# A fused transformer step on one core: one split of V per chunk, other pools and a later row load in the expert stage

## The chip, the cores and the metric

The kernel runs on one core of a Trainium2 chip. The metric is the device time of one execution in microseconds; the median of three runs of the kernel before is 3129.43 us (3128.04 to 3133.86). Besides the runs there is a profile of one execution, with every instruction of the engines (TensorE or PE, VectorE or DVE, ScalarE or ACT, GpSimd or POOL, SyncE or SP) and every DMA packet.

## The reference

Two networks run one after the other on 512 tokens of width 1024, all in float32. The first mixes neighbourhood attention and a gated recurrence and then has a PEER layer, the stage that the change touches; the second is two layers of convolution, attention and feed-forward. PEER, cut to what matters:

```python
def block(t):                                   # 128 tokens, width 1024
    q = (t @ wq).reshape(128, 8, 2, 128)        # 8 heads
    s = einsum('tpcd,pckd->tpck', q, sub_keys)
    # product keys: the 16 best of 128 x 128 experts per head, idx and gate g
    a = gelu(einsum('tpkd,td->tpk', u[idx], t))
    return einsum('tpk,tpkd->td', g * a, v[idx])
```

There are 16384 experts, each with a row of U and a row of V of 1024 numbers.

## The kernel before, in words

**Two ways for one sum.** Of the four tiles of 128 tokens, tile 0 takes the 128 chosen rows of U and V of each token by indirect DMA (`gathered`): 256 loads of 128 rows, 512 KB each, interleaved u, v, u, v. A u row is multiplied with the token's hidden row and summed on VectorE (line 1161), a v row is scaled and added to `accg` (line 1166). The ring of gathered rows has five buffers, and loads run four jobs ahead.

The other three tiles (384 tokens) go densely through all experts on TensorE, in 128 chunks of 128 experts. The U stage (`ahead`, `hidden`) multiplies each chunk of U with the hidden vectors, called the moving rows of U, pool `h2`, applies gelu, and stores the result, `act`, 128 x 384, to a DRAM tensor `Ad`. At the same time the routing is computed, and the gate of every token for every expert, mostly zeros, is written to a DRAM tensor `Wd`. The V stage, in `peer` from line 1055, then computes for each chunk e `(act * gate)^T @ V[e]` and sums over all 128 chunks in six PSUM banks (3 tiles x 2 halves).

**Split products.** A float32 product is made of three matmuls: each operand is split into a high part (a copy rounded to fp32r by ScalarE) and a low part (the difference, by VectorE), and high x high, high x low and low x high are summed. One chunk of V has 18 matmuls of 512 columns: 3 tiles x 3 parts x 2 halves.

**One chunk of the V stage** (`operands`, line 1377): SP loads `act` (192 KB) and V[e] (512 KB, tile `w`). VectorE multiplies act with the gates `Wr` (line 1390), ScalarE makes vh (1391) and sh (1392), VectorE makes vl (1393) and sl (1394). Then SP issues a sixth of the next group's gates (`spread_rows`, chunks 2 to 7 of each group of 8, while a next group is left). Then line 1397 calls `split`, which allocates vh and vl of the same names anew and computes both again from `w`, at lines 134 and 136; the matmuls read this second pair.

**Order.** For TensorE, VectorE and ScalarE the V stage runs in the order in which it is written (`manual_schedule`); SP's and POOL's instructions are placed by a planner, and each queue runs in order. After the operands of chunk e come the gather jobs that are due: what is left of them at the start of the stage is spread evenly over chunks 0 to 119, in pairs of one u and one v step. Then come the products of chunk e - 4 (`OPS_LAG`). Chunks 126 and 127 are held back and multiplied at the end, tile by tile (`TAIL`).

**Memory.** Pools are opened on the left or on the right of SBUF and reuse the space of pools that were closed; a tile in reused space waits, by itself, for the last users of the tiles that it lies on. `pm` (right) holds the stage's tiles: Wr two buffers, act six, vh, vl, sh, sl six each; `w` has four buffers in another pool. `ar` (left) holds the row `gt2r`, a modulation row loaded to all partitions by SP (`rows_of`, line 368); it is read after the stage, at line 1096, where the sums are scaled and added to X, and the tiles of the following norms lie in `pt` on the right, opened when `pm` is closed.

Of the kernel before, what the change touches and what calls it, by code (L numbers as in the profile page):

```python
# [8 lines left out]
FR = mybir.dt.float32r  # L9
# [13 lines left out]
TD = S - T0  # L23
# [5 lines left out]
VBUFS = 6  # L29
# [6 lines left out]
OPS_LAG = 4  # L36
TAIL = 2
# [15 lines left out]
def run(gen):  # L53
    while True:
        try:
            next(gen)
        except StopIteration as e:
            return e.value


def steps(gen, n):
    for _ in range(n):
        yield next(gen)


def weave(*gens):

    at = [[0.0, i, g] for i, g in enumerate(gens)]
    while at:
        cur = min(at, key=lambda x: (x[0], x[1]))  # L70
        try:
            cur[0] += next(cur[2])
        except StopIteration:
            at.remove(cur)
# [18 lines left out]
class Net:  # L93
# [931 lines left out]
    def peer(self):  # L1025
        nc, p = self.nc, self.p
        hh, hl = self.h2
        mv = ([hh[:, k] for k in range(KC)], [hl[:, k] for k in range(KC)])
        first = self.proj_first(self.ws, mv, lambda i: self.normed_half(i, [(hh, hl, self.a2)], 1e-6, self.sh2))
        self.finish = None  # L1030
        for name in ("wo", "st", "hca", "y", "pn"):
            self.shut(name)
        mk = self.pool("mk")
        self.mk = mk.tile([128, 2, 2, C], F32, name="mk")
        self.mv = mk.tile([128, 2, 2, C], F32, name="mv")
        self.open_stream()
        self.Wd = self.tc.dram_tile([TD // WT, 128, 128, WT], F32, name="Wd")
        self.Ad = self.tc.dram_tile([128, 128, TD], F32, name="Ad")
        pg = self.pool("pg")
        self.rows_natural(pg)  # L1040
        sc = self.queries(mv, first)
        pq = self.pool("pq", "right")
        pa = self.pool("pa")
        dense = tuple([x[:, T0:] for x in part] for part in mv)
        ahead = self.ahead(pa, dense)
        self.chosen = None
        gather = self.gathered(pg)
        with self.tc.manual_schedule(engines={mybir.EngineType.PE}):
            weave(self.route(pq, pg, sc), steps(ahead, 128 - REST), self.until_routed(gather))
        self.shut("pq")  # L1050
        self.shut("psc")
        run(ahead)
        self.shut("pa")
        self.shut("h2")
        pm = self.pool("pm", "right")
        ar = self.pool("ar")
        for i in range(GROUP - WLATE):
            self.spread_rows(pm, 0, i)
        rows = self.rows_of(3, "gt2r", ar)
        banks = [[self.bank() for _ in range(2)] for _ in range(3)]  # L1060
        ops = {}
        held = []
        left = self.gather_left
        done = 0
        E = mybir.EngineType
        with self.tc.manual_schedule(engines={E.PE, E.DVE, E.Activation}):
            for e in range(128 + OPS_LAG):
                if e < 128:
                    ops[e] = self.operands(pm, e)
                want = left * min(e + 1, 120) // 120  # L1070
                for _ in range(done, want):
                    next(gather, None)
                done = max(done, want)
                if e >= OPS_LAG:
                    x = e - OPS_LAG
                    if x < 128 - TAIL:
                        self.products(banks, range(3), [(x, ops.pop(x))])
                    else:
                        held.append((x, ops.pop(x)))
        run(gather)  # L1080
        for t in range(3):
            self.products(banks, [t], held)
        self.shut("pm")
        pt = self.xp = self.pool("pt", "right")
        nf = pt.tile([128, D], F32, name="nf")
        nc.scalar.dma_start(nf, self.rowb(p['normf'], D))
        self.ss = ss = self.sp.tile([128, 4, 2], F32, name="ssx")
        self.xh = {}
        self.ws = [self.first_weights(p['awin'], 2304, q) for q in range(2)]
        for t in range(4):  # L1090
            sq = self.sp.tile([128, 2], F32, name="ssp")
            for h in range(2):
                b = banks[t - 1][h] if t else self.accg[:, h * 512:(h + 1) * 512]
                hs = slice(h * 512, (h + 1) * 512)
                y = pt.tile([128, 512], F32, name="y2", bufs=2)
                nc.vector.tensor_tensor(out=y, in0=b, in1=rows[:, hs], op=OP.mult)
                nc.vector.tensor_tensor(out=self.X[:, t, hs], in0=self.X[:, t, hs], in1=y, op=OP.add)
                self.square_sum(self.X[:, t, hs], sq[:, h:h + 1], pt.tile([128, 512], F32, name="sqx", bufs=2))
            r = self.rstd(sq, 1e-6)
            for h in range(2):  # L1100
                hs = slice(h * 512, (h + 1) * 512)
                nc.vector.scalar_tensor_tensor(self.X[:, t, hs], self.X[:, t, hs], r, nf[:, hs], op0=OP.mult, op1=OP.mult)
                self.square_sum(self.X[:, t, hs], ss[:, t, h:h + 1], pt.tile([128, 512], F32, name="sqx", bufs=2))
            self.unit(t, 1e-5, 4)
        self.shut("ar")
        self.shut("pg")
# [270 lines left out]
    def operands(self, pm, e):  # L1377

        nc, p = self.nc, self.p
        n, j = divmod(e, GROUP)  # L1380
        if j == 0:
            self.Wr = self.Wn
        a = pm.tile([128, TD], F32, name="act", bufs=ABUFS)
        nc.sync.dma_start(a, self.Ad[e])
        v = self.st.tile([128, 2, 512], F32, name="w", bufs=WBUFS)
        nc.sync.dma_start(v.rearrange("p a b -> p (a b)"), p['V'][e])
        vh, vl = (pm.tile([128, 2, 512], FR, name=n, bufs=VBUFS) for n in ("vh", "vl"))
        sh, sl = (pm.tile([128, TD], FR, name=n, bufs=VBUFS) for n in ("sh", "sl"))
        a3 = a.rearrange("p (b t) -> p b t", t=WT)
        self.anchor = nc.vector.tensor_tensor(out=a3, in0=a3, in1=self.Wr[:, :, e % GROUP], op=OP.mult)  # L1390
        nc.scalar.activation(vh, v, AF.Copy)
        nc.scalar.activation(sh, a, AF.Copy)  # L1392
        nc.vector.tensor_tensor(out=vl, in0=v, in1=vh, op=OP.subtract)  # L1393
        nc.vector.tensor_tensor(out=sl, in0=a, in1=sh, op=OP.subtract)  # L1394
        if j >= WLATE and e < 128 - GROUP:
            self.spread_rows(pm, n + 1, j - WLATE)
        vh, vl = self.split(pm, v, [128, 2, 512], "v", bufs=TAIL + OPS_LAG)
        return sh, sl, vh, vl

    def spread_rows(self, pm, n, i):  # L1400
# [460 lines left out]
```

## Time and profile before

| what | value |
|---|---|
| median of 3 runs | 3129.43 us |
| the profiled execution | 3129.33 us, span 3127.5 us |
| TensorE busy in the span | 2937.5 us, 94% |
| VectorE busy | 2033.6 us, 65% |
| ScalarE busy | 1387.3 us, 44% |
| moved by DMA | 544.63 MB, mean 174 GB/s |
| V stage, 1338 to 1987 us | TensorE 569.24 us, VectorE 630.78, ScalarE 314.07, 325 GB/s |

Busy time is the union of an engine's instructions. PE is TensorE's matmuls, PEld its weight loads, SPq, ACTq and POOLq the parts of an engine that issue DMAs. In a timeline or a group, `[... <-X]` or `idle before ... <-X` is the time that the engine stood idle before it and the instruction that released it. The DMA share is the time that packets took over the time of the 16 DMA engines; packets that overlap count twice. A start is in us from the first instruction.

### The profile page before, as it was taken

How to read it: one execution, taken by the hardware profiler on the slowest of the kernel's cores; microseconds unless marked ns; L12 is line 12 of the kernel's file. 1: busy time of each engine (PE TensorE's matmuls, PEld its weight loads, DVE VectorE, ACT ScalarE, POOL GpSimd, SP SyncE). 2: the span in 40 equal slices, each digit the busy share in tenths (PEclk: the TensorE clock that was granted, in tenths of full speed). 3: DMA queues.
4: the chain of work that ended last, by engine and by line, in shares of the span. 5: the costliest groups of instructions: out<-in, count | busy, mean ns of one | idle time of the engine just before them, and what ended most of it. 6: DMA issues, size and time to landing. Idle time of an engine off the chain costs nothing.

```text
span 3127.5 us, 42558 instructions
## 1 busy us (share of the span) xinstructions
PE 2937.5 (94%) x16010; PEld 2488.1 (80%) x16010; DVE 2033.6 (65%) x3768; ACT 1387.3 (44%) x2404; POOL 458.0 (15%) x399
## 2 busy tenths in 40 slices
PE   7898998999999999978888888899999999999998
PEld 5787987899998999966666666678888887788887
DVE  5744496459999867679999999644433335543323
ACT  4233563343466667844444444533322234433222
POOL 2100000000111222224444443000000000000000
PEclk9999999999999999999999999899999999999999
DMA  6622202345666778899999998222333222123332
GB/s 251 226 69 78 62 1 95 108 133 193 225 231 218 267 263 290 294 311 337 342 338 337 341 341 306 87 71 90 101 99 97 95 88 66 51 88 96 100 102 81
DMA packets 262510, 544.63 MB, mean 174 GB/s; under 512 B 21904, under 2 KB 139936, under 8 KB 257952
## 3 DMA queue, kind: packets, MB, share of 16 engines
q1 hardware_dynamic: 200096, 350.28, 34.1%
q0 software_dynamic: 36896, 134.25, 12.6%
q10 hardware_dynamic: 25312, 57.39, 5.0%
q8 instruction: 125, 2.05, 0.3%
q14 instruction: 81, 0.66, 0.1%
HBM read 489.38 MB, written 52.45 MB: 173 GB/s over the span
## 4 chain that ended last, share of the span: by engine, by line
PE 53%; DVE 23%; issue 10%; DMA 2%; POOL 1%; ACT 1%; SPq 0%; POOLq 0%; ACTq 0%; DVEq 0%
PE bank L123 51%; DVE vl L1393 4%; DVE accg L1166 3%; DVE gr L1161 3%; DVE act L1390 2%; DVE sl L1394 2%; DVE wl L1350 1%; POOL gr L1142 1%; PE bank L608 1%; PE bank L1500 1%; DVE A L826 1%; DVE KX L802 1%; DVE QX L803 0%; DMA gr<-in_Un_dram,iu 0%; DVE tmp L1240 0%
## 5 line engine op out<-in xcount | busy, mean ns | idle before, releaser
L123 PE MATMUL bank<-hh,wl 128*128 128x512 f32 (+2 forms) x2304 | 837.0, 364 | 31.7 <-DVE wl L1350 21.2
L123 PE MATMUL bank<-hh,wh 128*128 128x512 f32 (+2 forms) x2304 | 840.5, 366 | 10.8 <-ACT wh L149 4.4
L123 PE MATMUL bank<-hl,wh 128*128 128x512 f32 (+2 forms) x2304 | 834.8, 362 | 1.8 <-DVE hl L273 1.1
L150 DVE TENSOR_TENSOR wl<-w,wh 128x1024 fp32r<-128x1024 f32 (+2 forms) x280 | 295.2, 1055 | 645.9 <-ACT wh L149 639.0
L149 ACT ACTIVATE wh<-w 128x1024 fp32r<-128x1024 f32 (+2 forms) x280 | 257.4, 920 | 746.1 <-PE bank L123 602.9
L123 PEld LDWEIGHTS bank<-hh,wl 128*128 128x128 f32 x2304 | 437.8, 190 | 89.9 <-DVE wl L1350 32.3
L123 PEld LDWEIGHTS bank<-hh,wh 128*128 128x128 f32 x2304 | 436.7, 190 | 64.8 <-ACT wh L149 5.0
L123 PEld LDWEIGHTS bank<-hl,wh 128*128 128x128 f32 x2304 | 437.8, 190 | 49.2 <-DVE hl L273 1.9
L1142 POOL DMA_INDIRECT gr<-in_V_dram,iv x128 | 212.4, 1660 | 588.1 <-DVE gr L1161 546.2
L123 PE MATMUL bank<-vl,sh 128*128 128x512 f32 x768 | 247.7, 404 | 42.9 <-DVE vl L136 42.8
L123 PE MATMUL bank<-vh,sh 128*128 128x512 f32 x768 | 245.4, 401 | 36.9 <-ACT vh L134 36.9
L123 PE MATMUL bank<-vh,sl 128*128 128x512 f32 x768 | 237.9, 391 | 0.0
L123 PEld LDWEIGHTS bank<-vl,sh 128*128 128x128 f32 x768 | 137.6, 188 | 105.7 <-DVE vl L136 82.0
L123 PEld LDWEIGHTS bank<-vh,sh 128*128 128x128 f32 x768 | 139.6, 188 | 89.8 <-ACT vh L134 63.5
L1142 POOL DMA_INDIRECT gr<-in_Un_dram,iu x128 | 165.9, 1296 | 295.1 <-DVE gr L1161 158.3
L1392 ACT ACTIVATE sh<-act 128x384 fp32r<-128x384 f32 x128 | 67.3, 526 | 309.1 <-DVE act L1390 309.1
L1349 ACT ACTIVATE wh<-w 128x1024 fp32r<-128x1024 f32 x128 | 135.4, 1058 | 142.3 <-PE bank L123 133.4
L1350 DVE TENSOR_TENSOR wl<-w,wh 128x1024 fp32r<-128x1024 f32 x128 | 156.1, 1220 | 62.1 <-ACT wh L1349 62.1
L123 PEld LDWEIGHTS bank<-vh,sl 128*128 128x128 f32 x768 | 144.5, 188 | 31.3
L217 POOL TENSOR_TENSOR r<-r,mhalf 128x1 f32<-128x1 f32 x37 | 21.7, 590 | 987.2 <-DVE r L216 979.8
L1161 DVE SCALAR_TENSOR_TENSOR gr<-gr,h 128x1024 f32<-128x1024 f32 x128 | 155.9, 1219 | 15.4 <-DMA gr<-in_Un_dram,iu 15.4
L1166 DVE SCALAR_TENSOR_TENSOR accg<-gr,wt,accg 128x1024 f32<-128x1024 f32 x127 | 162.7, 1281 | 0.4
(369 smaller groups left out, 5059.2 us busy)
## 6 DMA issues: line engine op xcount, KB each, us to landing
w<-in_U_dram SPq DMA_DIRECT2D x128, 512.0 KB
w<-in_V_dram SPq DMA_DIRECT2D x128, 512.0 KB
w<-in_wgu_dram SPq DMA_DIRECT2D x84, 512.0 KB
Ad<-act ACTq DMA_DIRECT2D x128, 192.0 KB
Wd<-W ACTq DMA_DIRECT2D x24, 1024.0 KB
Wr<-Wd SPq DMA_DIRECT2D x96, 256.0 KB
act<-Ad SPq DMA_DIRECT2D x128, 192.0 KB
w<-in_wdown_dram SPq DMA_DIRECT2D x44, 512.0 KB
```

The lines of the kernel that those rows point to most:

```text
L123: return self.nc.tensor.matmul(out, a, b, start=start, stop=stop)
L149: self.nc.scalar.activation(hi[:, :, :n], w[:, :, :n], AF.Copy)
L150: (self.low or self.nc.vector).tensor_tensor(out=lo[:, :, :n], in0=w[:, :, :n], in1=hi[:, :, :n], op=OP.subtract)
L1142: nc.gpsimd.indirect_dma_start(out=t, out_offset=None, in_=table, in_offset=bass.IndirectOffsetOnAxis(ap=idx, axis=0))
L1161: nc.vector.scalar_tensor_tensor(t, t, 1.0, self.h0, op0=OP.mult, op1=OP.mult, accum_out=dots[:, h, k:k + 1])
L1166: nc.vector.scalar_tensor_tensor(acc, t, wt[:, h, k:k + 1], acc, op0=OP.mult, op1=OP.add)
L1349: nc.scalar.activation(uh, w, AF.Copy)
L1350: nc.vector.tensor_tensor(out=ul, in0=w, in1=uh, op=OP.subtract)
L1390: self.anchor = nc.vector.tensor_tensor(out=a3, in0=a3, in1=self.Wr[:, :, e % GROUP], op=OP.mult)
L1392: nc.scalar.activation(sh, a, AF.Copy)
L1393: nc.vector.tensor_tensor(out=vl, in0=v, in1=vh, op=OP.subtract)
L1394: nc.vector.tensor_tensor(out=sl, in0=a, in1=sh, op=OP.subtract)
```

## The change

The call of `split` at line 1397 is deleted, so that the pair of lines 1391 and 1393 is the one that the matmuls read. The low parts vl and sl move to a pool of their own, `pl`, opened on the right ahead of `pm` as soon as the moving rows of U (`h2`) are closed; `pm` follows it with Wr, act, vh and sh. The pool `ar` and the load of `gt2r` move from the start of the stage to behind its last gather. The number of buffers stays six each.

```diff
--- before.py
+++ after.py
@@ -1052,11 +1052,10 @@
         run(ahead)
         self.shut("pa")
         self.shut("h2")
+        self.late = self.pool("pl", "right")
         pm = self.pool("pm", "right")
-        ar = self.pool("ar")
         for i in range(GROUP - WLATE):
             self.spread_rows(pm, 0, i)
-        rows = self.rows_of(3, "gt2r", ar)
         banks = [[self.bank() for _ in range(2)] for _ in range(3)]
         ops = {}
         held = []
@@ -1078,9 +1077,12 @@
                     else:
                         held.append((x, ops.pop(x)))
         run(gather)
+        ar = self.pool("ar")
+        rows = self.rows_of(3, "gt2r", ar)
         for t in range(3):
             self.products(banks, [t], held)
-        self.shut("pm")
+        for name in ("pm", "pl"):
+            self.shut(name)
         pt = self.xp = self.pool("pt", "right")
         nf = pt.tile([128, D], F32, name="nf")
         nc.scalar.dma_start(nf, self.rowb(p['normf'], D))
@@ -1384,8 +1386,8 @@
         nc.sync.dma_start(a, self.Ad[e])
         v = self.st.tile([128, 2, 512], F32, name="w", bufs=WBUFS)
         nc.sync.dma_start(v.rearrange("p a b -> p (a b)"), p['V'][e])
-        vh, vl = (pm.tile([128, 2, 512], FR, name=n, bufs=VBUFS) for n in ("vh", "vl"))
-        sh, sl = (pm.tile([128, TD], FR, name=n, bufs=VBUFS) for n in ("sh", "sl"))
+        vh, vl = (x.tile([128, 2, 512], FR, name=n, bufs=VBUFS) for x, n in ((pm, "vh"), (self.late, "vl")))
+        sh, sl = (x.tile([128, TD], FR, name=n, bufs=VBUFS) for x, n in ((pm, "sh"), (self.late, "sl")))
         a3 = a.rearrange("p (b t) -> p b t", t=WT)
         self.anchor = nc.vector.tensor_tensor(out=a3, in0=a3, in1=self.Wr[:, :, e % GROUP], op=OP.mult)
         nc.scalar.activation(vh, v, AF.Copy)
@@ -1394,7 +1396,6 @@
         nc.vector.tensor_tensor(out=sl, in0=a, in1=sh, op=OP.subtract)
         if j >= WLATE and e < 128 - GROUP:
             self.spread_rows(pm, n + 1, j - WLATE)
-        vh, vl = self.split(pm, v, [128, 2, 512], "v", bufs=TAIL + OPS_LAG)
         return sh, sl, vh, vl
 
     def spread_rows(self, pm, n, i):
```

## Rows read from the trace of the kernel before

**Rows 1.** Stretch; busy us of PE, PEld, DVE, ACT, POOL; granted clock; DMA share; GB/s.

```profile
1400.00:1900.00 500.00, 443.58 (x1796) 327.39 (x1797) 498.58 (x629) 241.88 (x304) 222.78 (x150) 1.00 0.98 341
```

**Rows 2.** Timeline of TensorE in the tail: start us, us, line, tiles, count.

```profile
1977.34 0.61 PE L123 MATMUL bank<-vh,sh 128*128 128x512 f32 x2
...
1985.50 0.61 PE L123 MATMUL bank<-vh,sh 128*128 128x512 f32 x2
```

**Rows 3.** Groups by line, V stage: busy us, mean ns | idle before <-releaser.

```profile
L123 PE MATMUL bank<-vl,sh 128*128 128x512 f32 x768 | 247.7, 404 | 42.9 <-DVE vl L136 42.8
...
L123 PE MATMUL bank<-vh,sh 128*128 128x512 f32 x768 | 245.4, 401 | 36.9 <-ACT vh L134 36.9
...
L136 DVE TENSOR_TENSOR vl<-w,vh 128x1024 fp32r<-128x1024 f32 x128 | 156.9, 1226 | 0.0
```

**Rows 4.** Timeline of VectorE and POOL, four chunks of the V stage.

```profile
1603.19 0.55 DVE L1390 TENSOR_TENSOR act<-act,Wr 128x384 f32<-128x384 f32 x1
...
1606.43 1.22 DVE L1161 SCALAR_TENSOR_TENSOR gr<-gr,h 128x1024 f32<-128x1024 f32 x1
...
1607.92 1.74 POOL L1142 DMA_INDIRECT gr<-in_V_dram,iv  x1 [2.23 <-DVE gr L1161]
...
1608.77 0.55 DVE L1390 TENSOR_TENSOR act<-act,Wr 128x384 f32<-128x384 f32 x1
...
1612.01 0.55 DVE L1390 TENSOR_TENSOR act<-act,Wr 128x384 f32<-128x384 f32 x1
...
1614.10 1.23 DVE L136 TENSOR_TENSOR vl<-w,vh 128x1024 fp32r<-128x1024 f32 x1
...
1615.24 1.22 DVE L1161 SCALAR_TENSOR_TENSOR gr<-gr,h 128x1024 f32<-128x1024 f32 x1
```

**Rows 5.** DMA issues from 1400 to 1900 us: count, KB each, median us to landing.

```profile
w<-in_V_dram SPq DMA_DIRECT2D x100, 512.0 KB
act<-Ad SPq DMA_DIRECT2D x99, 192.0 KB
Wr<-Wd SPq DMA_DIRECT2D x72, 256.0 KB
gr<-in_V_dram,iv POOLq DMA_INDIRECT x78, 7.0
gr<-in_Un_dram,iu POOLq DMA_INDIRECT x72
```

**Rows 6.** Stretches of one group of chunks, columns as in rows 1.

```profile
1625.00:1640.00 15.00, 13.28 (x55) 10.05 (x56) 15.00 (x20) 7.87 (x11) 6.68 (x5) 1.00 1.07 356
...
1640.00:1650.00 10.00, 8.76 (x36) 6.28 (x35) 10.00 (x13) 3.69 (x6) 4.92 (x5) 1.00 1.03 399
...
1650.00:1660.00 10.00, 9.08 (x39) 6.87 (x39) 10.00 (x14) 6.03 (x8) 4.22 (x3) 1.00 0.87 287
...
1625.00:1630.00 5.00, 4.19 (x17) 3.17 (x18) 5.00 (x7) 1.84 (x4) 2.46 (x3) 1.00 1.07 326
```

**Rows 7.** Timeline of the start of the V stage [idle before <-releaser].

```profile
1332.77 4.53 SPq L1406 DMA_DIRECT2D Wr<-Wd  x6
...
1342.83 0.33 SPq L371 DMA_DIRECT2D gt2r<-Rd  x1
...
1347.64 0.56 DVE L1390 TENSOR_TENSOR act<-act,Wr 128x384 f32<-128x384 f32 x1 [15.32 <-DMA act<-Ad]
```

**Rows 8.** Chain of waits at the start of the V stage: start us, us, what.

```profile
1339.01 3.74 DMA Ad<-act
...
1343.26 4.36 DMA act<-Ad
```

**Rows 9.** Line 1386, V's loads: ns min/median/max, first and last start us.

```profile
L1386 SPq DMA_DIRECT2D w<-in_V_dram x128: 328/333/3145, 1320.4 to 1964.2; - x128
```

**Rows 10.** Timeline of VectorE at the end of the V stage.

```profile
1979.33 0.69 DVE L1096 TENSOR_TENSOR y<-accg,gt2r 128x512 f32<-128x512 f32 x1
...
1986.61 0.69 DVE L1096 TENSOR_TENSOR y<-accg,gt2r 128x512 f32<-128x512 f32 x1 [6.59 <-PE bank L123]
```

## The prediction

> **What bounds the kernel now.** I read the busy times by stretch first. Between 1400 and 1900 us, in the stage that multiplies by V, VectorE is busy 498.6 of 500 us; TensorE reads 443.6 and ScalarE 241.9 [rows 1]. A matmul's row there is longer than its pitch, since neighbours overlap, so TensorE's own pace has to come from starts: in the stage's tail, where it waits for nothing, 36 matmuls lie between the starts 1977.34 and 1985.50 [rows 2]. That is 0.227 us each, 4.08 us for the 18 of one chunk, and 522 us for 128 chunks; the stage, 1338 to 1987 us, takes 649.
>
> The groups by line then say whom TensorE waits for: 42.9 us ahead of the products with vl, released by VectorE's line 136, and 36.9 us ahead of those with vh, released by ScalarE's line 134 [rows 3]. Both lines are the second split of V: lines 1391 and 1393 have already made a pair that nobody reads. Line 136 alone is 128 x 1226 ns = 157 us of VectorE [rows 3].
>
> Last, VectorE's order in time. A chunk with a pair of gather steps runs from 1603.19 to 1608.77, 5.58 us; one without from 1612.01 to 1615.24, 3.23 us [rows 4]. In 500 us 100 V tiles are loaded and 78 + 72 = 150 rows gathered [rows 5], so 75 of 100 chunks have the pair, 6 of 8. Eight chunks are 6 x 5.58 + 2 x 3.23 = 39.9 us, as 500 us for 100 confirm. VectorE, with no gap, sets the pace of chunks 0 to 119; after that no gathers are left and TensorE runs at its own.
>
> **The second split goes.** Line 136 takes from 1614.10 to 1615.24, 1.14 us start to start [rows 4]. A chunk with gathers falls to 4.44 us, one without to 2.09; eight take 6 x 4.44 + 2 x 2.09 = 30.8 us. ScalarE's second copy lay beside VectorE's work, and an engine at 48% sets nothing before or after; it counts zero. TensorE's eight chunks are 8 x 4.08 = 32.6 us. So VectorE stops being the bound, and by these engines alone TensorE would be next, 7.3 us faster per eight chunks.
>
> **What is late next: the transfers.** The DMA engines move 341 GB/s over the 500 us, at a share of 0.98 [rows 1]. That share can't be read as full: packets overlap, and it passes 1 where the engines are pressed, 1.03 with 399 GB/s from 1640 to 1650, while the next 10 us have 0.87 with 287 GB/s [rows 6]. There is room, and I size it. A group of eight chunks moves 8 x (512 + 192) KB of V and act, 6 x 256 KB of Wr (line 1396 makes six calls) and 12 x 512 KB of gathered rows, in all 13.63 MB (sizes in [rows 5]). The 15 us with one group's Wr loads, in short packets, read 356 GB/s, 5.34 MB [rows 6]; the 3.77 MB beside Wr's 1.57 take 9.45 us at 399 GB/s, so Wr takes 5.55 us. A group needs 12.06 MB / 399 GB/s = 30.2 us plus 5.55, in all **35.8 us**: above TensorE's 32.6, below the 39.9 of now. My forecast is that the transfers become the bound and a group gains 39.9 - 35.8 = 4.1 us. Fifteen groups (chunks 0 to 119) give **62 us**.
>
> Two corrections I let cancel. Four V tiles and up to five gathered ones lie in SBUF when the stage starts, 4.7 MB or 12 us of transfer that needn't keep pace. Against it, engines kept full without a hole are an ideal: 3% lost of 15 x 35.8 us is 16 us, 5% is 27 us.
>
> [...]
>
> **Pools and the moved row load.** Today the stage begins late. SP has issued six Wr loads by 1337.3, then stands at the gt2r load, which goes out only at 1342.83 [rows 7]: its pool lies on the U stage's act tiles, whose last store (1339.01 plus 3.74 us) has to land [rows 8]. Behind it in SP's queue are the act loads; the first goes at 1343.26, lands after 4.36 us [rows 8], and VectorE's first product, at 1347.64, has waited 15.3 us for it [rows 7], with ScalarE's sh and TensorE behind. With the row load gone, act can follow Wr at 1337.3; with the same 4.36 us the first product starts at 1341.7, 6 us earlier. If the first act load must itself wait for the last store (nothing here shows whether), only the row load's place is gained, 1 us. I take **5 us**, nearer to what the chain of waits shows. vl and sl now lie on the moving rows of U, so their first writes wait for U's last matmul, a new wait; that matmul is over before the store at 1339.01, so the act tile is later still. Were it last, sl, vl and the first gather steps stand behind it on VectorE, below 1 us.
>
> At the other end SP issues gt2r behind V's last load, which goes out at 1964.2 [rows 9], and ahead of the awin weights. Its reader, line 1096, starts at 1979.33 [rows 10]: 15 us of cover for 0.33 us of issue [rows 7] and 0.52 MB / 399 GB/s = 1.3 us of transfer. Cost nothing; without cover about 5 us, as act took from issue to use. The tiles of the norm that follows now lie on vl and sl rather than on pm. Today the second y waits 6.6 us for TensorE [rows 10]; it may come free sooner, or the first one later: -3 to +1 us, taken as zero.
>
> **Sum.** 62 + 5 = 67 us off the stage; the 1140 us behind it (1987 to 3127.5) move as they are. The profiled execution took 3129.33 us for a span of 3127.5, and the median is 3129.43, so I forecast a span of 3060 and a time of **3062 us**.
>
> **Rivals.**
> A, the forecast (chance 0.60): 3045 to 3093 by the two corrections, the start and the tail.
> B, TensorE becomes the bound (0.09): 32.6 us a group, 15 x 7.3 + 5 = 115 us, time 3014. For it: the tiles loaded ahead. Against it: 13.63 MB in 32.6 us is 418 GB/s, over the 399 of the pressed stretch. [...]
> C, the long-run rate is below that of 10 us bursts (0.12): at the 356 GB/s of 1625 to 1640 a group takes 38.3 us, 15 x 1.6 + 5 = 29 us, time 3100. That row's share of 1.07 speaks for it, the 399 behind it against. [...]
> D, the gather ring becomes the wait (0.09). It has five buffers, so a V row's load goes out after the u step two pairs earlier: step at 1606.43, load at 1607.92 [rows 4], 1.49 us. It is used 1.14 us (a u step) into its own pair, so two chunks can't be shorter than landing plus 0.35 us. By the median of 7.0 us [rows 5] that is 7.4, under the 8.95 of two chunks at 35.8 us a group. If full queues push landing to 10 us, 1.4 us are lost in four chunks, 42 us in all: time 3104.
> E, slower (0.04): gathers and Wr, now always together, hold the engines at the 326 GB/s of 1625 to 1630 [rows 6]. A group takes 41.8 us, 1.9 more than now: 15 x 1.9 - 5 = 23 us lost, time 3152. It decides below 13.63 MB / 39.9 us = 342 GB/s. Against it stands the 399 of the stretch behind.
> F, no change (0.06): 341 GB/s is already the ceiling, a share of 0.98 means what it says, and only the start gains: 3124. The hole of 287 GB/s speaks against it. The second split would be gone, and VectorE would idle where it now works.
>
> A difference under 0.2%, 6 us, can't be told from none here. A to D are faster (0.90), F is the same (0.06), E slower (0.04). The range, 3014 to 3106, takes in B, C and D and leaves out E, F and a little below.
>
> **What would show it.** Lines 134 and 136 have no vh and vl left. In the same 500 us VectorE's busy share falls from 99.7% to about 86% (30.8 of 35.8), the rate rises to about 380 GB/s, and the first waits in a chunk are for landings (act, w or gr ahead of VectorE and ScalarE). VectorE's first product starts near 1342 and TensorE's last near 1919. gt2r goes out near the end. Wrong would be: about 341 GB/s with VectorE idle (E, F), VectorE waiting for gr alone beside DMA holes (D), TensorE without waits at 4.08 us a chunk (B), or a first product not before 1346.

## The result and the profile after

The changed kernel takes 3046.62 us (median of four runs, 3045.89 to 3050.66) against 3130.91 us before; the ratio is 0.9733, with a 95% interval of 0.9717 to 0.9750. The forecast was 3062 us, and the measured time lies 15 us below it, inside the range that was given. The profiled execution has a span of 3044.8 us, 82.7 less than before.

The span splits at four points: U's last matmul, VectorE's first product with act, the end of the last gather step, and the end of TensorE's last matmul with V.

| stretch, us | before | after | gained |
|---|---|---|---|
| to the start of U's last matmul | 1338.1 | 1337.4 | 0.7 |
| from there to the first product with act | 9.5 | -0.2 | 9.7 |
| from there to the end of the last gather step (chunks 0 to 119) | 603.6 | 540.3 | 63.3 |
| from there to the end of TensorE's last matmul with V | 35.8 | 34.2 | 1.6 |
| from there to the end of the span | 1140.5 | 1133.1 | 7.4 |

The forecast had 62 us for the third line, 5 for the second and nothing for the last. Busy times of the changed kernel in five stretches, with the columns of [rows 1]:

```profile
1340.00:1380.00 40.00, 40.00 (x178) 32.88 (x176) 36.46 (x50) 14.26 (x20) 18.91 (x14) 1.00 1.05 385
1400.00:1900.00 500.00, 480.56 (x2004) 369.76 (x2003) 430.69 (x581) 172.34 (x233) 221.82 (x155) 0.99 1.02 370
1400.00:1500.00 100.00, 97.12 (x412) 75.05 (x411) 88.99 (x123) 34.66 (x47) 48.55 (x34) 1.00 1.05 385
1700.00:1800.00 100.00, 94.08 (x390) 71.63 (x389) 82.10 (x113) 31.86 (x43) 45.89 (x32) 0.98 1.02 369
...
1725.00:1730.00 5.00, 5.00 (x23) 4.11 (x23) 5.00 (x8) 1.76 (x3) 3.61 (x3) 0.99 0.82 264
```

Against [rows 1] VectorE falls from 498.6 to 430.7 of 500 us, 86%, and the rate rises from 341 to 370 GB/s with the share at 1.02. In the first stretch TensorE has no hole, which fits the V tiles and gathered rows loaded ahead. Later the rate sags from 385 to 369 GB/s. The sag is made of holes: between 1700 and 1800 us the three 5 us stretches from 1725 to 1735 and from 1760 read 264, 332 and 257 GB/s, and the other seventeen average 384. Ahead of the first hole VectorE has stood 4.85 us for ScalarE's vh, which had itself waited 5.55 us for V to land:

```profile
1720.72 1.23 DVE L1395 TENSOR_TENSOR vl<-w,vh 128x1024 fp32r<-128x1024 f32 x1 [4.85 <-ACT vh L1393]
```

Meanwhile it frees no buffer: SP's loads of V wait 5.9 us for vl between 1720 and 1728, and POOL's next gather, at 1723.83, has waited 11.6 us for VectorE's u step. Who waits for whom, by groups of the stage (idle before <- releaser, as in [rows 3]):

```profile
L123 PE MATMUL bank<-vh,sh 128*128 128x512 f32 x759 | 242.9, 401 | 20.2 <-ACT sh L1394 19.4
L123 PE MATMUL bank<-vl,sh 128*128 128x512 f32 x758 | 241.1, 400 | 2.0
...
L1395 DVE TENSOR_TENSOR vl<-w,vh 128x1024 fp32r<-128x1024 f32 x128 | 156.1, 1220 | 68.1 <-ACT vh L1393 67.1 <-issue 1.0
...
L1393 ACT ACTIVATE vh<-w 128x1024 fp32r<-128x1024 f32 x127 | 133.7, 1053 | 164.3 <-DMA w<-in_V_dram 152.1 <-PE bank L123 6.9 <-issue 5.2
L1168 DVE SCALAR_TENSOR_TENSOR accg<-gr,wt,accg 128x1024 f32<-128x1024 f32 x98 | 125.4, 1280 | 4.8 <-DMA gr<-in_V_dram,iv 4.5
```

The 42.9 and 36.9 us of [rows 3] have become 2.0 and 20.2. Read from the transfers upward: ScalarE's vh waits 152 us for V to land, VectorE's vl waits 67 us for vh, and TensorE is left with 22 us of waiting. A landing now stands where VectorE's second split stood.

The start, by instruction (SP's queue, VectorE, TensorE; compare [rows 7]):

```profile
1319.72 2.45 SPq L1388 DMA_DIRECT2D w<-in_V_dram  x2
1322.26 9.54 SPq L1407 DMA_DIRECT2D Wr<-Wd  x6
1332.20 1.28 SPq L1386 DMA_DIRECT2D act<-Ad  x3
...
1337.27 0.56 DVE L1392 TENSOR_TENSOR act<-act,Wr 128x384 f32<-128x384 f32 x1 [5.62 <-DMA act<-Ad]
...
1337.45 0.34 PE L123 MATMUL bank<-hh,wl 128*128 128x384 f32 x1
1338.44 0.73 PE L123 MATMUL bank<-vh,sh 128*128 128x512 f32 x2 [0.65 <-ACT sh L1394]
...
1348.33 5.16 SPq L371 DMA_DIRECT2D gt2r<-Rd  x1
```

SP loads Wr from 1322.26, ahead of V's third tile; before it went at 1332.77, behind the fourth. So act follows at 1332.20 and TensorE goes from U to V with 0.65 us of waiting. The planner did not leave gt2r at the end: it goes out at 1348.33, in the stage's first chunks.

The end, the changed kernel first and the kernel before second (compare [rows 10]):

```profile
1903.18 0.69 DVE L1098 TENSOR_TENSOR y<-accg,gt2r 128x512 f32<-128x512 f32 x1 [3.24 <-PE bank L123]
...
1911.14 0.61 PE L123 MATMUL bank<-vh,sl 128*128 128x512 f32 x2
...
1914.40 1.00 PE L267 MATMUL bank<-ident,xh 128*128 128x128 f32 x7 [2.64 <-DVE xh L253]
```

```profile
1986.41 0.61 PE L123 MATMUL bank<-vh,sl 128*128 128x512 f32 x2
...
1996.69 1.54 PE L267 MATMUL bank<-ident,xh 128*128 128x128 f32 x6 [9.66 <-DVE xh L253]
```

The second y starts 8 us before TensorE's last matmuls, where it used to start with them. Tile 0's norm then runs beside the held products, and TensorE stands for 2.6 us behind V instead of 9.7.

### The profile page after: what moved, and what is told of

Same layout as the page of the kernel before. It is cut to its first block, busy times and chain, and to the rows that moved or that the text cites. A ratio compares the mean times of both kernels' runs of the same rounds, so it can differ in the third digit from the quotient of the medians.

```text
span 3044.8 us, 42380 instructions
## 1 busy us (share of the span) xinstructions
PE 2921.2 (96%) x16010; PEld 2493.4 (82%) x16010; DVE 1888.4 (62%) x3640; ACT 1268.0 (42%) x2276; POOL 445.7 (15%) x399
## 4 chain that ended last, share of the span: by engine, by line
PE 54%; DVE 15%; DMA 10%; issue 8%; POOL 1%; ACT 1%; SPq 0%; POOLq 0%; DVEq 0%; ACTq 0%
PE bank L123 52%; DMA w<-in_V_dram 7%; DVE accg L1168 2%; DVE vl L1395 2%; DMA Wr<-Wd 1%; DVE wl L1352 1%; DVE sl L1396 1%; DMA act<-Ad 1%; POOL gr L1144 1%; PE bank L608 1%; DVE act L1392 1%; DVE gr L1163 1%; PE bank L1501 1%; DVE KX L802 1%; DVE A L826 1%
## 5 line engine op out<-in xcount | busy, mean ns | idle before, releaser
L1144 POOL DMA_INDIRECT gr<-in_V_dram,iv x128 | 206.3, 1612 | 524.1 <-DVE gr L1163 475.6
L123 PE MATMUL bank<-vh,sh 128*128 128x512 f32 x768 | 245.6, 401 | 20.2 <-ACT sh L1394 19.4
L1144 POOL DMA_INDIRECT gr<-in_Un_dram,iu x128 | 159.7, 1248 | 298.8 <-DVE gr L1163 160.2
L1393 ACT ACTIVATE vh<-w 128x1024 fp32r<-128x1024 f32 x128 | 134.8, 1053 | 164.3 <-DMA w<-in_V_dram 152.1
L1395 DVE TENSOR_TENSOR vl<-w,vh 128x1024 fp32r<-128x1024 f32 x128 | 156.1, 1220 | 68.1 <-ACT vh L1393 67.1
```

Of the source, the lines that this page charges most:

```text
L123: return self.nc.tensor.matmul(out, a, b, start=start, stop=stop)
L1144: nc.gpsimd.indirect_dma_start(out=t, out_offset=None, in_=table, in_offset=bass.IndirectOffsetOnAxis(ap=idx, axis=0))
```

## The experiments

Each was timed beside the kernel before on the same chip. My theory: the second split made VectorE the bound, without it the transfers are, and start and tail come from pools and row load.

**One part at a time.** The first deletes the second split alone:

```diff
-        vh, vl = self.split(pm, v, [128, 2, 512], "v", bufs=TAIL + OPS_LAG)
```

> The kernel before without line 1397 alone (pools and row load as before). Theory 1 (the second split carries the stage, start and tail come from pools and row load): the stretch from VectorE's first product with act to its last gather step shrinks from 603.6 us to about 540, as in the changed kernel; the first product stays near 1347 and the stretch from the last matmul with V to the end near 1140 us; time about 3067. Rival (the start and tail gains are the split's own, since fewer VectorE and ScalarE instructions stand there): time about 3047, first product near 1337, 1133 us behind the stage.

Measured: 3067.89 us, ratio 0.9801 (0.9785 to 0.9817), as my theory had it. VectorE is as free as in the changed kernel, and the rate as high:

```profile
1400.00:1800.00 400.00, 381.91 (x1608) 295.55 (x1606) 342.75 (x469) 134.81 (x183) 184.55 (x132) 0.99 1.04 382
```

The second adds the later row load:

```diff
-        ar = self.pool("ar")
-        rows = self.rows_of(3, "gt2r", ar)
...
         run(gather)
+        ar = self.pool("ar")
+        rows = self.rows_of(3, "gt2r", ar)
```

> Line 1397 deleted and the row load moved behind the gathers, vl and sl still in pm. If the moved row load makes the start (my prediction's reason): first product near 1337 to 1342, time about 3058 to 3062, tail as before (1140 us). If the pools make it: first product still near 1346, time about 3066.

Measured: 3059.95 us, ratio 0.9781 (0.9758 to 0.9804). The time is that of the first reading; the first product, at 1347.1, is near that of the second, since U's last matmul itself came 3.6 us later in this profile than in the kernel before.

The third has the split deleted and the pools, with the row load where it was:

```diff
+        self.late = self.pool("pl", "right")
         pm = self.pool("pm", "right")
         ar = self.pool("ar")
...
+        vh, vl = (x.tile(..., name=n, bufs=VBUFS) for x, n in ((pm, "vh"), (self.late, "vl")))
+        sh, sl = (x.tile(..., name=n, bufs=VBUFS) for x, n in ((pm, "sh"), (self.late, "sl")))
```

> Line 1397 deleted and vl, sl in the pool over the moving rows of U, the row load at the start as before. If the pools carry the tail: 1133 us from the last matmul with V to the end, as in the changed kernel, whatever the start does. If they carry the start too: first product near 1337, time about 3047. If the row load carries the start: first product near 1346, time about 3055.

Measured: 3056.61 us, ratio 0.9765 (0.9748 to 0.9781). Start and tail are those of the whole change, and yet it is 10 us slower: 5 us in the gather phase, and most of the rest because U's last matmul came 4.6 us later in this profile.

The fourth is the changed kernel with the second split put back:

```diff
+        vh, vl = (x.tile(..., name=n, bufs=VBUFS) for x, n in ((pm, "vh"), (self.late, "vl")))
+        nc.scalar.activation(vh, v, AF.Copy)
+        nc.vector.tensor_tensor(out=vl, in0=v, in1=vh, op=OP.subtract)
         return sh, sl, vh, vl
```

> The changed kernel with the second split put back (V split twice, into the new pools). Theory 1: VectorE is full again, 39.9 us per eight chunks; only start (10 us) and tail (7 us) are gained: about 3113. Rival (a free buffer for each chunk's vh and vl, or the new order of SP's queue, is what sped the chunks up, not VectorE's time): about 3050.

Measured: 3118.82 us, ratio 0.9963 (0.9950 to 0.9975), 6 us above what I expected, most of it in the tail.

The fifth swaps the two pools:

```diff
-        self.late = self.pool("pl", "right")
         pm = self.pool("pm", "right")
+        self.late = self.pool("pl", "right")
```

> The changed kernel with the two pools opened in the other order: pm next to the right edge, on the moving rows of U, and pl behind it. If the start and the tail come from which tiles lie at the edge (pl there lets Wr load before V's third tile, and lets the norm's tiles start before TensorE ends): both are lost, first product about 9 us behind U's last matmul's start less the row load's 5, 1140 us behind the stage, time about 3060. If a pool of their own for vl and sl is what counts, wherever it lies: 3047.

Measured: 3058.27 us, ratio 0.9754 (0.9738 to 0.9771). The time is near the 3060 of the first reading, but half of the distance to the changed kernel is U's last matmul, 5.9 us later here.

The stretches of the first table in each of these profiles; U's last matmul starts between 1337.4 and 1343.4 in them, so the start is counted from it. That spread is older than the edits: U's first activation already starts between 684.5 and 690.2 us.

| kernel | U's last matmul to first product | gather phase | behind TensorE's end |
|---|---|---|---|
| before | 9.5 | 603.6 | 1140.5 |
| split alone | 9.9 | 537.1 | 1141.4 |
| split, row load | 5.3 | 536.9 | 1139.8 |
| split, pools | -0.4 | 545.6 | 1133.1 |
| pools, row load, V split twice | 0.3 | 603.5 | 1138.5 |
| pools in the other order | 5.1 | 540.9 | 1132.8 |
| the whole change | -0.2 | 540.3 | 1133.1 |

The columns have three causes. The gather phase belongs to the split: 537 to 546 us without it and 603.5 with it, whatever the pools do. With the second split back, VectorE is full again in the new pools, at the 339 to 341 GB/s of before:

```profile
1400.00:1900.00 500.00, 443.54 (x1794) 326.69 (x1793) 498.56 (x627) 243.48 (x305) 221.75 (x150) 1.00 0.98 339
```

The tail belongs to the pools, and goes with the second y: it starts 0.4 us ahead of TensorE's end in the old pool and 7.5 to 8.6 us ahead in the new ones. With V split twice it starts only 1.8 us ahead, after 5.3 us of waiting for TensorE, and the tail gains 2 us. In the other order the gain stays, so a pool of their own for vl and sl is what counts, and that half of my expectation was wrong. Which tile the second y used to wait for, no run shows.

The start has two causes. Without the second split, the row load's move takes it from 9.9 to 5.3; here is SP's queue, what its act load waits for and VectorE's first product, with the split gone and the row load moved, in the old pool:

```profile
1324.01 12.28 SPq L1386 DMA_DIRECT2D w<-in_V_dram  x4
1336.38 4.96 SPq L1405 DMA_DIRECT2D Wr<-Wd  x6
1344.63 1.33 SPq L1384 DMA_DIRECT2D act<-Ad  x3
```

```profile
SPq L1384 <- DMA Ad<-act: 3.2, 1, 3.2
```

```profile
1347.08 0.56 DVE L1390 TENSOR_TENSOR act<-act,Wr 128x384 f32<-128x384 f32 x1 [11.15 <-DMA act<-Ad]
```

act follows Wr, but Wr still stands behind four V tiles, whose buffers come free only as the U stage ends (in the kernel before their loads wait 17.3 us, in four waits, for VectorE's wl), and the first act load then waits 3.2 us for a store of U's act to land, the next to last by the chain of waits (issued at 1338.47, landed after 6.09 us). With pl at the edge the planner puts Wr ahead of the third V tile, with or without the row load's move, and act, at 1332.20 in the changed kernel, goes ahead of the last two stores. With pm at the edge Wr goes late, and act again waits 3.2 us for a store:

```profile
1325.65 12.29 SPq L1388 DMA_DIRECT2D w<-in_V_dram  x4
1338.03 4.36 SPq L1407 DMA_DIRECT2D Wr<-Wd  x6
1345.59 1.29 SPq L1386 DMA_DIRECT2D act<-Ad  x3
```

So pl at the edge brings the other 5 us and makes the row load's move nearly redundant at the start. The move pays behind it. Without it, in the new pools, SP's queue stands at gt2r with V's next loads behind:

```profile
SPq L371 <- DMA Ad<-act: 6.6, 1, 6.6
```

The rate is 292 GB/s from 1350 to 1360 us there, for 382 in the changed kernel, and the gather phase is 5.3 us longer. Why the planner orders SP's queue so, and which tile makes an act load wait for a store, is not shown.

**Less to move.** Wr is loaded for two groups only, in the changed kernel and then in the kernel before:

```diff
-        if j >= WLATE and e < 128 - GROUP:
+        if j >= WLATE and n == 0:
```

> The changed kernel with the gates Wr loaded for the first two groups of chunks only; later groups use the second group's again, so the sums of tiles 1 to 3 are not the reference's. 84 loads of 256 KB go, all else stays. Theory 1 (the transfers bound the stage): without Wr a group needs 30.2 us of transfer, under TensorE's 32.6, so the gather phase falls from 540 us to about 500 and the time to about 3006; TensorE is then the bound. Rival (TensorE's waits come from the order of the queues or the buffers, not from the transfers' rate): within 10 us of the changed kernel, about 3040 to 3047.

Measured: 3000.94 us, ratio 0.9577 (0.9561 to 0.9593). TensorE's waits are gone, here by groups of the stage and for 400 us of it:

```profile
L123 PE MATMUL bank<-vl,sh 128*128 128x512 f32 x768 | 236.6, 389 | 0.1
L123 PE MATMUL bank<-vh,sh 128*128 128x512 f32 x768 | 236.5, 389 | 0.5 <-ACT sh L1394 0.5
```

```profile
1400.00:1800.00 400.00, 400.00 (x1767) 331.31 (x1766) 392.99 (x536) 154.92 (x209) 229.29 (x154) 1.00 1.01 386
```

From TensorE's first matmul with V to its last are 523 us, 4.09 us a chunk. VectorE's gather steps run ahead of it and end after 473 us, not the 500 that I expected. Only Wr's loads were taken away, so they bounded the changed stage; their places in SP's queue went with their bytes, and this run alone does not part the two.

> The kernel before with the gates Wr loaded for the first two groups of chunks only (the sums of tiles 1 to 3 are not the reference's), no other edit: less to move, no new wait. Theory 1 (before the change VectorE bounds the stage and the transfers have room): the gather phase stays at 603 us, time 3125 to 3133. Rival (the transfers bounded it together with VectorE, at a share of 0.98): the phase falls with the changed kernel's, by 20 us or more.

Measured: 3130.77 us against 3130.41, ratio 0.9998 (0.9988 to 1.0007). The same loads taken from the kernel before give nothing:

```profile
1400.00:1900.00 500.00, 443.64 (x1796) 327.03 (x1795) 498.87 (x628) 242.36 (x303) 222.94 (x150) 1.00 0.89 301
```

301 GB/s instead of 341, and VectorE as full as ever: a share of 0.98 was no bound.

**More to move.** ScalarE stores a part of act that nobody reads:

```diff
         nc.scalar.activation(sh, a, AF.Copy)
+        if e < 120:
+            nc.scalar.dma_start(self.Xd[e], a[:, :256])
```

> The kernel before, and in chunks 0 to 119 ScalarE also stores 128 KB of act to a DRAM tensor that nobody reads. Theory 1: VectorE bounds the stage and the DMA engines have about 4 us of room in a group of eight chunks; the stores take 8 x 128 KB / 399 GB/s = 2.6 us of it, so the time stays within 10 us of 3130. Rival (the engines are full already at 341 GB/s): 15 x 2.6 = 39 us slower, 3170.

> The changed kernel with the same stores of 128 KB a chunk. Theory 1: the transfers bound the stage now, so each of the 15 groups takes about 2.6 us more: 39 us slower than the changed kernel, about 3086. Rival (TensorE or the order of waits bounds it): within 10 us of 3047.

Measured: 3212.53 us, ratio 1.0248 (1.0231 to 1.0266), on the kernel before, and 3079.18 us, ratio 0.9836 (0.9819 to 0.9853), on the changed one. The second came out near its 39 us, 33 more than the changed kernel. The first fits neither theory. SP's waits between 1400 and 1800 us say why, the kernel before first:

```profile
SPq L1385 <- DMA Xd<-act: 265.7, 62, 7.4
```

```profile
SPq L1387 <- DMA Xd<-act: 196.7, 69, 6.7
```

The store holds act's buffer, and the next act load waits for it at the head of SP's queue, V's loads behind it. I added a wait, not only bytes, in both kernels; neither run decides anything about the rate. The rate can stand higher than the changed kernel's 378 GB/s, though: with the stores it is 389 over the same 400 us.

**A version that beats both.** If transfers bound the V stage and the U stage has room, gathers belong earlier:

```diff
-GATHER = (13.0, 13.0, 9.0, 6.0, 4.5)
+GATHER = (13.0, 13.0, 7.5, 5.0, 3.6)    # first try
+GATHER = (13.0, 10.0, 6.0, 4.0, 3.0)    # second try
```

> The changed kernel with the gathers paced closer during routing (pace values 13, 13, 7.5, 5, 3.6 for 13, 13, 9, 6, 4.5), so that 54 u steps instead of 46 stand ahead of the first chunk of V. If the transfers bound the V stage, each pair moved takes 1.05 MB / 375 GB/s = 2.8 us off it: 8 pairs, 22 us, time about 3025, as long as the U stage hides them (its rate is near 290 GB/s and VectorE has a quarter of its time free). Rival (the U stage has no room either and gives it back): 3047 or more.

Measured: 3052.67 us, ratio 0.9755 (0.9738 to 0.9771). The gather phase fell from 540 to 518 us, the 22 expected, but U's last matmul starts at 1361.5 instead of 1337.4: all given back, as the rival had it. The V stage's part says more about the bound: gathered rows go through POOL's queue, so this try leaves SP's loads in the stage as they were. It takes VectorE's steps on these rows away too, but the run without Wr kept those. What both took away is transfers, and each made the stage shorter.

> The same, further: pace values 13, 10, 6, 4, 3, 65 u steps ahead of the first chunk of V. 19 pairs by 2.8 us are 53 us, but TensorE's own 4.08 us a chunk allows about 45 off the stage: time about 3003 if the U stage hides them all. Rival: the U stage's rate would go to about 360 GB/s and VectorE to nearly full; if they delay U's chunks, half or more is given back, 3020 to 3050.

Measured: 3031.28 us, ratio 0.9675 (0.9659 to 0.9692). The gather phase is 485.5 us, 55 less than in the changed kernel, and U's end comes 37 us later. Two stretches of it, U stage and V stage:

```profile
1050.00:1300.00 250.00, 231.76 (x1401) 228.09 (x1402) 197.84 (x258) 157.81 (x318) 91.04 (x58) 0.96 0.83 294
1400.00:1800.00 400.00, 400.00 (x1766) 331.43 (x1765) 341.73 (x472) 148.12 (x200) 170.31 (x116) 1.00 1.05 380
```

TensorE is full in the V stage, with Wr's loads in place. In the U stage it falls short (231.8 of 250 us) though VectorE is at 79% and the rate at 294 GB/s: there the room I counted on wasn't to be had. The time lies in the rival's range, but not by the rival's means, which were 360 GB/s and a nearly full VectorE. TensorE's matmuls wait for VectorE's wl, 12.0 us and 21.4 us behind 1050 us in the two tries against 4.5 in the changed kernel, and 24.4 and 23.5 against 14.8 ahead of it: 17 and 26 us more, of 24 and 37 lost. A gather step that stands ahead of wl in VectorE's queue is a likely reason, not one that was tested. Of the kernels that load all of Wr this is the fastest: a ratio of 0.9675 to the kernel before, where the change has 0.9733, with intervals that do not meet.

## Why the prediction was right

**The bound before.** VectorE, by the second split: shown. The split alone moves the gather phase from 603.6 to 537.1 us, and Wr's loads taken from the kernel before move nothing.

**The next bound.** The transfers, not TensorE: shown by the run without Wr, in which the waits vanish and TensorE's 4.08 us a chunk remain, together with the two tries that moved gathered rows out of the stage. A group of eight chunks was forecast at 35.8 us; 540.3 us over 15 groups are 36.0. The two corrections that I let cancel can both be seen, 40 us without a hole in TensorE at the start and a rate that holes pull from 384 to 369 GB/s later, 4% in those 100 us; that they cancelled to 1 us is luck in part, since neither was measured alone.

**Sum.** The stage's term of 62 us measured 63.3. What made the forecast 15 us too slow are two small terms, 12 us together. The start was 9.7 us for 5: the step "act can follow Wr at 1337.3" held SP's order ahead of it fixed, and SP's order changed. With the row load's move alone the start gained 4.6 us, near the 5, but not by that step: act did not follow Wr, it waited 3.2 us for a store to land, the case that the prediction named and priced at 1 us. That the size came out is luck. Nothing ahead of the result told that pl would move Wr. The tail was 7.4 us for "-3 to +1, taken as zero": the wait that could go was 6.6 us in [rows 10], and I bounded the gain by less than the wait. Tile 0's whole norm stood behind that y in VectorE's queue, so the chain moved with it.

**Checks named ahead.** VectorE's share at 86% was right to the percent, the landing of V was among the waits named, TensorE's last matmul came at 1911 for 1919 and VectorE's first product at 1337 for 1342. One was wrong: gt2r goes out early. The rate of 370 GB/s for 380 has its reason in the window, which now runs past the last gather step at 1877.6; from 1400 to 1800 us it is 378.

**Rivals.** B fell: TensorE waits, and its pace is reached only where transfers leave the stage, Wr's loads or the second try's gathered rows. C fell by size: the long-run rate does lie below the 399 of a 10 us burst, but at 378 GB/s, not at the 356 on which it rested, and by holes. D fell: in the V stage VectorE's accumulation of gathered rows waits 4.5 us for them to land, in all 98 instructions together, where the kernel before has no such wait. E and F fell with the time.

## What to carry to other kernels

A share of 0.98 on the DMA engines bounded nothing here: without Wr's later loads it was 0.89, and the kernel before took the same time. The rate of a pressed stretch against that of the whole group gave the next bound to within 1 us in 36 here, two errors cancelling. Price a step's wait with all that stands behind it in its engine's queue, not by the instruction that waits. And when a pool moves, compare the order of the queues that a planner fills before crediting the edit that was meant to change it.

## What was not expected of the hardware

Behind one short wait TensorE ran slower than ahead of it. In the changed kernel it stands for 1.55 us ahead of 1604.60, and then:

```profile
1604.60 0.73 PE L123 MATMUL bank<-vh,sh 128*128 128x512 f32 x2 [1.55 <-ACT sh L1394]
1605.45 1.12 PE L123 MATMUL bank<-vl,sh 128*128 128x512 f32 x2
1606.36 1.05 PE L123 MATMUL bank<-vh,sl 128*128 128x512 f32 x2
1607.22 1.05 PE L123 MATMUL bank<-vh,sh 128*128 128x512 f32 x2
```

```profile
1604.00:1609.00 5.00, 4.29 (x11) 3.08 (x12) 4.40 (x6) 2.02 (x4) 0.00 (x0) 0.66 1.05 392
```

Pairs start 0.85 to 0.91 us apart instead of 0.45, and the granted clock over these 5 us is 0.66: 1.00 in the first of them, 0.80 from 1605 to 1606 and 0.50 from 1606 to 1609. Not every wait is followed by this: one of 1.10 us ahead of 1758.13 is followed by starts 0.85 and 0.57 us apart and then by 0.45 to 0.47 again, and the clock reads 1.00 from 1755 to 1760 us. Whether the wait is the reason, and what it costs the kernel, whose TensorE waits for transfers anyway, no run shows.
